# Query chunks split ahead of the second norm, transposes replaced by scaling matmuls, and modulation products kept back, in a decoder layer

## The chip, the cores and the metric

The kernel runs on one core of a Trainium2 chip. The metric is the device time of one execution in microseconds (us). Three runs of the kernel before took 1857.24, 1858.06 and 1858.55 us, a median of 1858.06.

The engines, by the names that the profile uses: PE is TensorE's matmul (PEld its weight load), DVE is VectorE, ACT is ScalarE, POOL is GpSimd, and SP is SyncE, which issues most of the loads. Each engine takes its instructions in the order in which they stand in its own list; an instruction that waits holds back all that stand behind it on that engine.

## What is computed

One layer of a decoder for 256 tokens of width 2048, all in float32. The parts that matter here:

```python
mod = (c_act @ w_ada[l] + b_ada[l]).reshape(B, 6, 1, D)
shift1, scale1, gate1, shift2, scale2, gate2 = jnp.moveaxis(mod, 1, 0)
h = rmsnorm(x, g_norm_mix[l]) * (1.0 + scale1) + shift1
q_a, ..., v_r, g_r = split_cols(h @ w_in[l], IN_SIZES)
o_nsa = ...                       # sparse attention, 16 heads of 64
o_ret = retention(..., g_r, ...)  # 8 heads of 128, silu(g_r) * normed output
x = x + gate1 * (jnp.concatenate([o_nsa, o_ret], axis=-1) @ w_out[l])
h2 = rmsnorm(x, g_norm_ffn[l]) * (1.0 + scale2) + shift2
x = x + gate2 * peer_ffn(h2, ...) # query product with peer_w_q, top-k, expert rows u and v
return rmsnorm(x, g_norm_final)
```

## The kernel before

Weights are streamed from HBM in chunks of 1 MB (128 partitions by 2048 floats). `load` issues such a chunk on SP into one of four `raw` buffers. `split_to` makes two parts of it: ACT copies it, rounded, to `whi` (L157), and DVE subtracts that from the chunk to get the remainder `wlo` (L158), each in two halves. Activations are kept split in the same way, as `hh` and `hl` in one tile `act`. A product is then three matmuls: hi by hi, hi by lo and lo by hi. There are two `whi` and two `wlo` buffers, so that two split chunks can stand ready.

The modulation `c_act @ w_ada` has 96 chunks (six vectors j of 16 chunks k). Each is a `raw` buffer that one DVE instruction multiplies with the broadcast row `crow` and sums (`ada_chunk`, L198, "the product"). They are spread over the whole first half of the program by `background(pace)`: a table PACE says how many of them stand behind each unit of other work (PACE["out"] behind each chunk of the output projection).

The stages around the change, in order of time:

- `d_pair` makes two rows of 128 of q and k of the input projection, in a bank `psD`. Its sum goes to `xT` by a DVE add (L430).
- `n_tile` makes 256 tokens by 512 columns in two banks `psN` from four chunks of 24 matmuls (L453): for the retention's values (`ret_v`), for its gates (`ret_gate`, which ACT turns to `sg` by a Silu, L633; there is one buffer `sg` for both halves of the heads), and later for the output projection (`woutN`, 16 chunks).
- `ret_head` runs a retention head: scores `scr`, decay `at` (L649), output `por`, its norm (L661 to L665). `ret_out` multiplies with the gate (`orr`, L672) and transposes (`psT`). `o_split` splits the output into `act` for the output projection (L677, L678).
- The output projection: four column tiles q. After each, for both token halves tt, DVE multiplies the bank with the gate row `g1` (`xg`, L719) and adds the residual (L720; the residual x is loaded into `xT`'s place, called x2, by eight loads on SP), and ACT squares and sums (L722).
- The second norm: `token_rstd` (a sum and a scaling on DVE, L215 and L216, and the power on POOL, L221), then eight DVE scalings `xn` (L731), 32 transposes on PE (`psX`, L736), evictions with the modulation's scale and shift on DVE and ACT in turn (L740, L742), and the split into `hh` (ACT, L743) and `hl` (DVE, L744).
- Then the first pools are closed and others opened. The 16 query chunks `wqT` follow: the first two in one loop (`t_blocks`, banks `psA`, L237 and L238), the others one by one, with ten more modulation products, the scores against the sub-keys, and the top-k on DVE. Behind these come the expert rows u (`psU`, L1111) and v (`acc`, L990), on PE without stop to the end.

The order of all instructions on an engine comes from a scheduler, by priorities (`tc.high_priority(offset=...)`) and readiness; `tc.keep_in_program_order` pins an instruction to the place in which it was written.

Of the kernel before, what the change touches and what calls it, by code (L numbers as in the profile page):

```python
# [30 lines left out]
PACE = dict(A=2, C=0.5, B=0.8, pair=1.5, tile=1.4, head=1.4, out=0.75)  # L31
# [84 lines left out]
def body(ctx, tc, a, out, dbg=None, stop=None):  # L116
# [8 lines left out]
    base = ctx.enter_context(tc.tile_pool(name="base", bufs=1))  # L125
    strm = []
# [26 lines left out]
    def split_to(r, hi, lo, parts=1):  # L153
        n = hi.shape[-1] // parts
        for i in range(parts):
            sl = slice(i * n, i * n + n)
            nc.scalar.copy(hi[:, sl], r[:, sl])  # L157
            nc.vector.tensor_sub(lo[:, sl], r[:, sl], hi[:, sl].bitcast(F32))  # L158

# [35 lines left out]
    def ada_chunk(j, k, crow):  # L195

        r = load(a["adaT"][j, k])
        nc.vector.scalar_tensor_tensor(r, r, 1.0, crow, op0=OP.mult, op1=OP.mult, accum_out=modc[:, j, k:k + 1])  # L198
# [29 lines left out]
    def t_blocks(pool, src_chunks, tags=("A", "A"), parts=2, dst=None):  # L228

        if dst:  # L230
            split_to(load(src_chunks[0]), *dst, parts)
        w = [dst] if dst else [split(load(c), parts=parts) for c in src_chunks]
        ps = [pool.tile([P, 2, S], F32, name="psA", tag=t) for _, t in zip(w, tags)]
        for k in range(KB):
            sl = slice(k * P, (k + 1) * P)
            for p_, (hi, lo) in zip(ps, w):
                nc.tensor.matmul(p_, hi[:, sl], act[:, k], start=k == 0, stop=False, skip_group_check=True)  # L237
                nc.tensor.matmul(p_[:, 1, :], lo[:, sl], hh[:, k, :], start=False, stop=k == KB - 1, skip_group_check=True)  # L238
        return ps

    def t_block(pool, src_chunk, tag="A", **kw):
        return t_blocks(pool, [src_chunk], (tag,), **kw)[0]

    def summed(ps, dst, n=S):

        nc.scalar.copy(dst, ps[:, 1, 0:n])
        nc.vector.tensor_add(dst, dst, ps[:, 0, 0:n])
# [31 lines left out]
    with ExitStack() as fctx:  # L279
        strm.append((fctx.enter_context(tc.tile_pool(name="strm", bufs=1)), dict(raw=4, whi=2, wlo=2)))  # L280
        fp = fctx.enter_context(tc.tile_pool(name="front", bufs=1))
        ones = fp.tile([P, P], F32, name="ones")
# [20 lines left out]
        kcv = fp.tile([P, 4, 2, P], F32, name="kcv", tag="f4k", bufs=2)  # L303
        ksw = [fp.tile([P, S], F32, name=f"ksw{i}") for i in range(4)]
        vsw = fp.tile([P, 2, 512], F32, name="vsw")
# [4 lines left out]
        pp = fctx.enter_context(tc.tile_pool(name="fpsum", bufs=2, space=PS))  # L310
# [17 lines left out]
        def background(n=1):  # L328
# [3 lines left out]
            for _ in range(n):  # L332
# [3 lines left out]
                ada_chunk(j, k, crow)  # L336
                if j == 0:
                    nc.vector.tensor_add(modc[:, 0:2, k], modc[:, 0:2, k], b_col[:, 0:2, k])
                    nc.vector.tensor_scalar(scol[:, 0, k:k + 1], modc[:, 1, k:k + 1], 1.0, g_mix[:, k:k + 1],
                                            op0=OP.add, op1=OP.mult)  # L340
                elif 1 < j < 5 and k == KB - 1:
                    nc.vector.tensor_add(modc[:, j, :], modc[:, j, :], b_col[:, j, :])
                    if j == 4:
                        nc.vector.scalar_tensor_tensor(scol[:, 1, :], modc[:, 4, :], 1.0, g_ffn, op0=OP.add, op1=OP.mult)
# [70 lines left out]
        kT2 = fp.tile([P, 4, 2, P], F32, name="kT2", tag="f4k", bufs=2)  # L415
# [27 lines left out]
        def n_tile(i, src="winN", tag="A", pace="tile"):  # L443
            ps = [pp.tile([P, 512], F32, name="psN", tag=tag) for _ in range(2)]
            for c in range(4):
                hi, lo = split(load(a[src][i, c].rearrange("p k e -> p (k e)")))
                for kk in range(4):
                    k = 4 * c + kk
                    w = slice(kk * 512, (kk + 1) * 512)
                    for tt in range(2):  # L450
                        ts_ = slice(tt * P, (tt + 1) * P)
# [910 lines left out]
```

## Time and profile before

| | |
|---|---|
| median of three runs | 1858.06 us |
| the profiled execution | 1856.91 us, its span 1855.2 us |
| matmuls on PE busy | 1793.1 us (97%) |
| DVE busy | 1485.7 us (80%) |
| ACT busy | 708.7 us (38%) |
| HBM read | 644.97 MB, 350 GB/s over the span |

A page of the profile has the busy times of the engines over the span, the chain of work that ended last (followed back from the last instruction, at each step to what released it), the costliest groups of instructions, and the waits. A row of a timeline reads: start, duration, engine, line, operation, what is written from what, and in brackets the engine's idle time before it with what ended it. A row of stretches reads: the stretch, its length, the busy time and count of PE, PEld, DVE, ACT and POOL, the granted clock of TensorE (1.00 is full), the DMA engines' busy share and GB/s. A row of waits reads: who waited, for whom, the sum in us, how often, the longest. A group's row reads: the line, engine, operation, names and shapes, how many, then busy us and mean ns, then the idle time before them.

### The profile page before, as it was taken

The page shows a single profiled execution, that of the slowest core. Times are in us where ns is not written, and L with a number is a line of the kernel's source. Part 1 is how long each engine was busy: PE and PEld are TensorE (multiplying, and loading weights), DVE is VectorE, ACT ScalarE, POOL GpSimd, SP SyncE. Part 2 cuts the span into 40 slices and gives each one's busy share as a digit, 9 for nine tenths or more (in the row PEclk, how much of TensorE's full clock was granted, in tenths as well). Part 3 has the DMA queues.
Part 4 walks back from the last instruction along what each step waited for, and adds up shares of the span by engine and source line. Part 5 has one row for each costly group of instructions (what it writes and reads, how often), then busy time and mean ns, then how long its engine had stood idle before and what let it go on. Part 6 is the DMA issues. An engine that isn't in the chain of part 4 may idle for free.

```text
span 1855.2 us, 28510 instructions
## 1 busy us (share of the span) xinstructions
PE 1793.1 (97%) x11264; PEld 1571.5 (85%) x11264; DVE 1485.7 (80%) x2336; ACT 708.7 (38%) x1284; POOL 366.1 (20%) x259
## 2 busy tenths in 40 slices
PE   5899999999889999999999999999999999999997
PEld 4899878797767899999997777779999998777775
DVE  7988889889779999586498999983555558998878
ACT  3444453745435421021045555541111114555554
POOL 1000001011010012211124434420111114544210
PEclk9999899999999999999999999999999999999999
DMA  8989887889887799999889999989999989999992
GB/s 341 409 320 362 313 308 292 342 302 334 318 338 279 278 322 364 424 366 376 332 346 386 423 420 416 409 355 425 367 345 359 354 316 404 426 421 403 388 316 99
DMA packets 94616, 653.96 MB, mean 353 GB/s; under 512 B 11409, under 2 KB 11633, under 8 KB 18449
## 3 DMA queue, kind: packets, MB, share of 16 engines
q1 hardware_dynamic: 66818, 467.78, 65.2%
q0 software_dynamic: 27664, 184.37, 25.3%
q8 instruction: 88, 1.44, 0.3%
q14 instruction: 46, 0.38, 0.1%
HBM read 644.97 MB, written 4.22 MB: 350 GB/s over the span
## 4 chain that ended last, share of the span: by engine, by line
PE 87%; DVE 7%; DMA 3%; issue 1%; ACT 1%; POOL 0%; SPq 0%; ACTq 0%; POOLq 0%; DVEq 0%
PE acc L990 31%; PE psU L1111 28%; PE psN L453 8%; PE psD L354 4%; PE psA L237 3%; PE bkB L354 2%; DMA raw<-in_adaT 2%; PE psA L238 1%; PE pg L1096 1%; DVE raw L198 1%; DVE wlo L158 1%; PE bkC L354 1%; PE bvB L406 1%; DMA raw<-in_winA 1%; PE pT L552 1%
## 5 line engine op out<-in xcount | busy, mean ns | idle before, releaser
L1111 PE MATMUL psU<-xT,raw 128*128 128x160 f32 x4096 | 569.5, 300 | 0.0
L1111 PEld LDWEIGHTS psU<-xT,raw 128*128 128x128 f32 x4096 | 558.3, 190 | 0.4
L990 PE MATMUL acc<-whi,cc 128*128 128x512 f32 x1512 | 369.1, 391 | 0.0
L990 PEld LDWEIGHTS acc<-whi,cc 128*128 128x128 f32 x1512 | 283.8, 188 | 70.0 <-issue 1.5
L967 DVE TENSOR_TENSOR wlo<-raw,whi 128x2048 fp32r<-128x2048 f32 x126 | 288.1, 2287 | 55.1 <-issue 47.4
L990 PE MATMUL acc<-wlo,cc 128*128 128x512 f32 x1008 | 254.2, 392 | 0.8 <-DVE wlo L967 0.6
L964 ACT CAST whi<-raw 128x2048 fp32r<-128x2048 f32 x126 | 240.7, 1911 | 0.5 <-DMA raw<-in_v 0.5
L198 DVE SCALAR_TENSOR_TENSOR raw<-raw,crow 128x2048 f32<-128x2048 f32 x96 | 219.0, 2283 | 19.7 <-DMA raw<-in_adaT 19.6
L157 ACT CAST whi<-raw 128x1024 fp32r<-128x1024 f32 (+1 forms) x174 | 168.5, 1018 | 167.1 <-DMA raw<-in_winA 32.4
L158 DVE TENSOR_TENSOR wlo<-raw,whi 128x1024 fp32r<-128x1024 f32 (+1 forms) x174 | 200.6, 1181 | 24.2 <-ACT whi L157 23.8
L990 PEld LDWEIGHTS acc<-wlo,cc 128*128 128x128 f32 x1008 | 161.5, 161 | 63.8 <-DVE wlo L967 3.1
L453 PE MATMUL psN<-whi,act 128*128 128x512 f32 x512 | 166.9, 402 | 1.4 <-ACT act L677 0.7
L1117 DVE TENSOR_TENSOR X<-X,ge 128x160 f32<-128x160 f32 (+19 forms) x94 | 25.8, 276 | 162.7 <-ACT ge L1116 160.5
L1113 ACT ACTIVATE X<-psU 128x160 f32<-128x160 f32 (+19 forms) x102 | 25.6, 251 | 315.6 <-PE psU L1111 299.6
L453 PEld LDWEIGHTS psN<-whi,act 128*128 128x128 f32 x512 | 95.9, 189 | 25.6 <-issue 1.7
L453 PE MATMUL psN<-wlo,act 128*128 128x512 f32 x256 | 103.3, 404 | 3.4 <-DVE wlo L158 3.4
L953 ACT CAST cc<-X 128x192 fp32r<-128x192 f32 x126 | 44.0, 352 | 148.1 <-PE acc L990 147.5
L237 PE MATMUL psA<-act,whi 128*128 128x512 f32 x240 | 87.2, 404 | 3.8 <-ACT whi L157 3.8
L806 POOL DMA_INDIRECT rows<-in_urow,sx x32 | 67.1, 2097 | 105.3 <-DVE rows L847 100.4
L806 POOL DMA_INDIRECT s<-in_urow,sx x26 | 53.9, 2072 | 120.6 <-DVE s L847 86.5
L354 PE MATMUL psD<-act,whi 128*128 128x256 f32 x384 | 75.4, 294 | 0.6 <-ACT whi L157 0.6
L969 ACT CAST cc<-cc 128x64 fp32r<-128x64 f32 x126 | 30.4, 243 | 117.2 <-DVE cc L954 117.2
(363 smaller groups left out, 2551.0 us busy)
## 6 DMA issues: line engine op xcount, KB each, us to landing
raw<-in_u SPq DMA_DIRECT2D x128, 1024.0 KB
raw<-in_v SPq DMA_DIRECT2D x128, 1024.0 KB
raw<-in_adaT SPq DMA_DIRECT2D x96, 1024.0 KB
raw<-in_winN SPq DMA_DIRECT2D x16, 1024.0 KB
raw<-in_woutN SPq DMA_DIRECT2D x16, 1024.0 KB
raw<-in_wqT SPq DMA_DIRECT2D x16, 1024.0 KB
raw<-in_winB SPq DMA_DIRECT2D x16, 832.0 KB
raw<-in_winD SPq DMA_DIRECT2D x12, 1024.0 KB
```

The source lines that it names most:

```text
L157: nc.scalar.copy(hi[:, sl], r[:, sl])
L158: nc.vector.tensor_sub(lo[:, sl], r[:, sl], hi[:, sl].bitcast(F32))
L198: nc.vector.scalar_tensor_tensor(r, r, 1.0, crow, op0=OP.mult, op1=OP.mult, accum_out=modc[:, j, k:k + 1])
L237: nc.tensor.matmul(p_, hi[:, sl], act[:, k], start=k == 0, stop=False, skip_group_check=True)
L354: nc.tensor.matmul(bank[:, b, :], x[:, w], y[:, k, :], start=k == k0 and n == 0 and first, stop=k == k1 - 1 and n == 2, skip_group_check=True)
L453: nc.tensor.matmul(ps[tt], x[:, k, ts_], y[:, w], start=k == 0 and j == 0, stop=k == KB - 1 and j == 2)
L806: pin(nc.gpsimd.indirect_dma_start(out=r, out_offset=None, in_=src, in_offset=bass.IndirectOffsetOnAxis(ap=o, axis=0)))
L953: inorder(nc.scalar.copy(ch, xb(j)))
L964: inorder(nc.scalar.copy(hi, r))
L967: nc.vector.tensor_sub(lo[:, i:i + n], r[:, i:i + n], hi[:, i:i + n].bitcast(F32))
L990: return nc.tensor.matmul(acc[c][0:m], x, w[:, c[1] * 512:(c[1] + 1) * 512], start=jj == 0 and n == 0, stop=jj == HALF - 1 and n == 2 - c[ ...
L1111: nc.tensor.matmul(ps, w[:, k * P:(k + 1) * P], xT[:, k, 0:TU], start=k == 0, stop=k == KB - 1)
```

## The change

1. The first three query chunks are loaded and split in the last column tile of the output projection. Their five parts stand in a pool `pre` (tile `w01`) that is opened where the attention's tiles (now in a pool `attn`) were, once that is closed behind the last `o_split`; the sixth takes the place of `crow`. So that this can be, the residual x is loaded to `xr`, in the place of `oT`, behind the last `o_split`.
2. One PSUM pool serves the whole kernel, with the same bank pairs.
3. In the last column tile the two token halves of the last two chunks are written one after the other (`apart=2`), and each half has its own `token_rstd`.
4. `xn` is gone: instead of transposing scaled rows, PE multiplies a slice of `xr` with a diagonal of the token half's factors (`dgs`, `turn_`). Eviction is as before; the split into `hh` and `hl` is made for two k at a time.
5. The matmuls of the first two query chunks are written between the turns, pinned in that order; the third chunk's stand behind them.
6. A modulation product (j of 2 or more) is kept back: its chunk is loaded where it was, and the DVE instruction stands pinned behind the next chunk's split.
7. PACE["out"] is 1.25 instead of 0.75. The ten products in the query loop stand at chunks 3 to 12 instead of 0 to 9, and each later query chunk is loaded and split one chunk ahead.

```diff
-PACE = dict(A=2, C=0.5, B=0.8, pair=1.5, tile=1.4, head=1.4, out=0.75)
+PACE = dict(A=2, C=0.5, B=0.8, pair=1.5, tile=1.4, head=1.4, out=1.25)
...
     def split_to(r, hi, lo, parts=1):
...
             nc.vector.tensor_sub(lo[:, sl], r[:, sl], hi[:, sl].bitcast(F32))
+        while pend_ada:
+            pend_ada.pop(0)(tc.keep_in_program_order)
...
     def ada_chunk(j, k, crow):
         r = load(a["adaT"][j, k])
-        nc.vector.scalar_tensor_tensor(r, r, 1.0, crow, op0=OP.mult, op1=OP.mult, accum_out=modc[:, j, k:k + 1])
+
+        def f(pin=lambda i: i):
+            pin(nc.vector.scalar_tensor_tensor(r, r, 1.0, crow, op0=OP.mult, op1=OP.mult, accum_out=modc[:, j, k:k + 1]))
+        return f
...
+def n_tile(i, src="winN", tag="A", pace="tile", apart=0):
...
             for c in range(4):
+                ws[c] = split(load(a[src][i, c].rearrange("p k e -> p (k e)")))
                 for kk in range(4):
                     for tt in range(2):
+                        if c < 4 - apart:
+                            mul(c, kk, tt)
                 background(pace)
+            for tt in range(2):
+                for c in range(4 - apart, 4):
+                    for kk in range(4):
+                        mul(c, kk, tt)
...
-        for q in range(4):
-            for tt in range(2):
-                nc.sync.dma_start(x2[:, tt, q * 512:(q + 1) * 512], a["x"][:, tt, q * 512:(q + 1) * 512])
         for k in range(12, KB):
             o_split(k, k + 1)
+        actx2.close()
+        w01 = fctx.enter_context(tc.tile_pool(name="pre", bufs=1)).tile([P, 5, D], F32R, name="w01")
+        xr = fp.tile([P, 2, D], F32, name="xr", tag="oT")
+        for q in range(4):
+            for tt in range(2):
+                nc.sync.dma_start(xr[:, tt, q * 512:(q + 1) * 512], a["x"][:, tt, q * 512:(q + 1) * 512])
...
             if q == 3:
                 background(len(todo))
+                settle()
+                w01 = [(w01[:, 2 * i, :], w01[:, 2 * i + 1, :] if i < 2 else fp.tile([P, D], F32R, name="w2l", tag="crow")) for i in range(3)]
+                for i, w in enumerate(w01):
+                    split_to(load(wq(i)), *w, 2)
...
+                    if q == 3:
+                        rcs.append(token_rstd(fp, ss[:, tt:tt + 1, :], 1, f"rc{tt}"))
+                        for rc in rcs if tt else []:
+                            dgs.append(fp.tile([P, P], F32, name=f"dg{len(dgs)}"))
+                            nc.vector.tensor_scalar(dgs[-1], ident, rc, None, op0=OP.mult)
...
-                    nc.vector.tensor_scalar(xn[:, tt, sl], x2[:, tt, sl], rc[:, tt:tt + 1], None, op0=OP.mult)
...
-                    nc.tensor.transpose(ps[:, tt, :], xn[:, tt, k * P:(k + 1) * P], ident)
...
+        def turn_(k, tt):
+            if tt == 0:
+                turned[k] = pp.tile([P, 2, 2, P], F32, name="psX", tag="TO"[k // 2 % 2])
+            for i in range(2):
+                tc.keep_in_program_order(nc.tensor.matmul(turned[k][:, i, tt, :], xr[:, tt, (k + i) * P:(k + i + 1) * P],
+                                                          dgs[tt], start=True, stop=True))
...
+            for tt in range(2):
+                for k in range(0, 8, 2):
+                    turn_(k, tt)
+            for k in range(0, KB, 2):
...
+                nc.scalar.copy(hh[:, k:k + 2, :], xT[:, k:k + 2, :])
+                nc.vector.tensor_sub(hl[:, k:k + 2, :], xT[:, k:k + 2, :], hh[:, k:k + 2, :].bitcast(F32))
+                for i in range(k, k + 2):
+                    t_block(first, w01[0:2], i, tc.keep_in_program_order)
+                if k + 8 < KB:
+                    for tt in range(2):
+                        turn_(k + 8, tt)
+        first += t_blocks(w01[2:], 2)
```

How the change moves instructions shows at three places. The first is PE's list where the output projection ends (psN) and the query product begins (psA); psX are the banks of the transposes or turns. Before:

```order
L453 MATMUL psN<-wlo,act 128x512
L453 MATMUL psN<-whi,act 128x512
L736 MATMUL psX<-small,xn 128x128 x32
L237 MATMUL psA<-act,whi 128x512
L238 MATMUL psA<-act,wlo 128x256
```

And now, where `dg` are the two diagonals and `w` the parts of the query chunks split ahead:

```order
L486 MATMUL psN<-whi,act 128x512
L791 MATMUL psX<-dg_4935,xr 128x128 x8
L791 MATMUL psX<-dg_4937,xr 128x128 x8
L260 MATMUL psA<-act,w_4277 128x512
L261 MATMUL psA<-act,w_4277 128x256
L260 MATMUL psA<-act,w_4277 128x512
L261 MATMUL psA<-act,w_4277 128x256
L260 MATMUL psA<-act,w_4277 128x512
L261 MATMUL psA<-act,w_4277 128x256
L260 MATMUL psA<-act,w_4277 128x512
L261 MATMUL psA<-act,w_4277 128x256
L791 MATMUL psX<-dg_4935,xr 128x128 x2
```

All 32 transposes stood ahead of the first query matmul; now 16 turns do, and the others stand two by two of each half between the query matmuls.

The second place is DVE's list at the same boundary. Before, from the last tile's residual on:

```order
L719 TENSOR_TENSOR xg<-psN,g_4420 128x512
L720 TENSOR_TENSOR xT<-xT,xg 128x512
L719 TENSOR_TENSOR xg<-psN,g_4420 128x512
L720 TENSOR_TENSOR xT<-xT,xg 128x512
L215 TENSOR_REDUCE rc<-ss 128x2
L216 TENSOR_SCALAR rc<-rc 128x2
L731 TENSOR_SCALAR xn<-xT,rc 128x512 x8
L740 TENSOR_SCALAR xT<-psX,scol,modc 128x256 x2
```

And now:

```order
L169 TENSOR_TENSOR w2l<-raw,w_4277 128x1024 x2
L772 TENSOR_TENSOR xg<-psN,g_4435 128x512
L775 TENSOR_TENSOR xr<-xr,xg 128x512
L233 TENSOR_REDUCE rc_4921<-ss 128x1
L234 TENSOR_SCALAR rc_4921<-rc_4921 128x1
L772 TENSOR_TENSOR xg<-psN,g_4435 128x512
L782 TENSOR_SCALAR dg_4935<-small,rc_4921 128x128
L775 TENSOR_TENSOR xr<-xr,xg 128x512
L233 TENSOR_REDUCE rc_4931<-ss 128x1
L234 TENSOR_SCALAR rc_4931<-rc_4931 128x1
L782 TENSOR_SCALAR dg_4937<-small,rc_4931 128x128
L802 TENSOR_SCALAR xT<-psX,scol,modc 128x256 x3
```

The first half's factors are made ahead of the second half's residual, and the splits of the three query chunks stand ahead of both. On PE the matmuls of the first half's last chunk end eight matmuls ahead of the last one.

The third place is DVE's list ahead of the two gate products (`orr<-orr,sg`) that release the one `sg` buffer for the second half of the heads. Before:

```order
L678 TENSOR_TENSOR act_70<-oT_90,act_70 128x2x256 x2
L158 TENSOR_TENSOR wlo_4161<-raw_4158,whi_4160 128x1024
L665 SCALAR_TENSOR_TENSOR bnb_3401<-bmv_3399,brs_3400 128x2
L158 TENSOR_TENSOR wlo_4161<-raw_4158,whi_4160 128x1024
L672 TENSOR_TENSOR orr_3377<-orr_3377,sg_3560 128x256
L678 TENSOR_TENSOR act_70<-oT_90,act_70 128x2x256
L198 SCALAR_TENSOR_TENSOR raw_4225,modc_65<-raw_4225,crow_95 128x2048
L672 TENSOR_TENSOR orr_3402<-orr_3402,sg_3560 128x256
```

And now:

```order
L169 TENSOR_TENSOR wlo_4294<-raw_4291,whi_4293 128x1024
L215 SCALAR_TENSOR_TENSOR raw_4228,modc_68<-raw_4228,crow_98 128x2048
L215 SCALAR_TENSOR_TENSOR raw_4324,modc_68<-raw_4324,crow_98 128x2048
L707 TENSOR_SCALAR brs_3377<-bmv_3376 128x2
L706 BN_AGGR bmv_3401<-bst_3400 128x2 x2
L722 TENSOR_TENSOR act_73<-oT_96,act_73 128x2x256
L707 TENSOR_SCALAR brs_3402<-bmv_3401 128x2
L169 TENSOR_TENSOR wlo_4332<-raw_4329,whi_4331 128x1024
L709 SCALAR_TENSOR_TENSOR bnb_3378<-bmv_3376,brs_3377 128x2
L709 SCALAR_TENSOR_TENSOR bnb_3403<-bmv_3401,brs_3402 128x2
L169 TENSOR_TENSOR wlo_4332<-raw_4329,whi_4331 128x1024
L215 SCALAR_TENSOR_TENSOR raw_4326,modc_68<-raw_4326,crow_98 128x2048
```

(The two gate products are the next two rows.) From the evacuation of the last projection pair (`xT<-cT,psD`) to the second gate product, two modulation products and four half splits stood before, and seven products and ten half splits stand now. Among them are already the splits of the output projection's first two chunks. On SP, the eight loads of x stood singly among the loads of `winN` and now stand together behind the sixth load of `woutN`.

More of the change, by code (lines that the diff above doesn't have):

```diff
@@ L226, in body, with t_blocks, t_block, summed @@
     hh, hl = act[:, :, 0, :], act[:, :, 1, :]
[L228 to L233, printed above, removed]
+    qbank = lambda i: f"b{(6, 7, 2, 3)[i % 4]}"
+    wq = lambda i: a["wqT"][i].rearrange("p k e -> p (k e)")
+    def t_blocks(w, i):
+        ps = [up.tile([P, 2, S], F32, name="psA", tag=qbank(i + n)) for n in range(len(w))]
         for k in range(KB):
[L235 to L238, printed above, removed]
-        return ps
[L241 to L247, printed above, removed]
+            t_block(ps, w, k)
+        return ps
+    def t_block(ps, w, k, pin=lambda i: i):
+        sl = slice(k * P, (k + 1) * P)
+        for p_, (hi, lo) in zip(ps, w):
+            pin(nc.tensor.matmul(p_, hi[:, sl], act[:, k], start=k == 0, stop=False, skip_group_check=True))
+            pin(nc.tensor.matmul(p_[:, 1, :], lo[:, sl], hh[:, k, :], start=False, stop=k == KB - 1, skip_group_check=True))
+    def summed(ps, dst, n=S, pin=lambda i: i):
+        pin(nc.scalar.copy(dst, ps[:, 1, 0:n]))
+        pin(nc.vector.tensor_add(dst, dst, ps[:, 0, 0:n]))
     def sumsq(wpool, kb, acc, src, tag="pr"):
@@ L732, in body @@
-        for k in range(KB):
-            with tc.high_priority(offset=(KB - k) * 10):
-                ps = pp.tile([P, 2, P], F32, name="psX", tag="TO"[k % 2])
-                for tt in range(2):
-                    nc.tensor.transpose(ps[:, tt, :], xn[:, tt, k * P:(k + 1) * P], ident)
-                t = xT[:, k, :]
-                ps = ps.rearrange("p t s -> p (t s)")
-                if k % 2:
-                    nc.vector.tensor_scalar(t, ps, scol[:, 1, k:k + 1], modc[:, 3, k:k + 1], op0=OP.mult, op1=OP.add)
-                else:
-                    nc.scalar.activation(t, ps, AF.Identity, bias=modc[:, 3, k:k + 1], scale=scol[:, 1, k:k + 1])
-                nc.scalar.copy(hh[:, k, :], t)
-                nc.vector.tensor_sub(hl[:, k, :], t, hh[:, k, :].bitcast(F32))
+                    nc.scalar.activation(sq, xr[:, tt, sl], AF.Square, accum_out=ss[:, tt, q:q + 1])
@@ new lines, in body @@
+                    if q == 3:
[3 more added lines that the diff above has]
+                            nc.vector.tensor_scalar(dgs[-1], ident, rc, None, op0=OP.mult)
+                nc.gpsimd.dma_start(x2d[:, tt, sl], xr[:, tt, sl])
+        first = [up.tile([P, 2, S], F32, name="psA", tag=qbank(i)) for i in range(2)]
@@ L758, in pair @@
             return t[:, 0, :], t[:, 1, :]
-        early = pair(0)
         X = []
```

150 lines of the change are left out of this document (87 added, 63 removed).

## The prediction

> **What bounds the kernel now.** First the page's busy times and the chain of work that ended last, then the busy times of chosen stretches.
>
> ```profile
> PE 1793.1 (97%) x11264; PEld 1571.5 (85%) x11264; DVE 1485.7 (80%) x2336; ACT 708.7 (38%) x1284; POOL 366.1 (20%) x259
> PE 87%; DVE 7%; DMA 3%; issue 1%; ACT 1%; POOL 0%; SPq 0%; ACTq 0%; POOLq 0%; DVEq 0%
> ...
> 446.00:545.00 99.00, 94.20 (x405) 74.76 (x404) 78.01 (x95) 40.43 (x60) 8.72 (x12) 0.98 0.88 328
> 545.00:576.00 31.00, 21.52 (x101) 17.00 (x101) 26.45 (x50) 16.79 (x37) 4.01 (x6) 0.78 0.71 274
> 660.00:703.00 43.00, 42.31 (x314) 41.49 (x313) 42.86 (x231) 10.46 (x21) 9.90 (x20) 1.00 0.92 327
> 703.00:760.00 57.00, 57.00 (x422) 57.00 (x422) 47.50 (x108) 7.54 (x18) 14.86 (x12) 1.00 0.95 388
> ```
>
> TensorE is the bound: 97% of the span, 87% of the chain. What can be won is its idle time, and that stands in two stretches that the change touches: 4.8 us of 99 in the output projection and 9.5 us of 31 behind it, where the granted clock is 0.78 besides. After 545 TensorE runs on with one small stop, so what is won or lost before is carried to the end. TensorE's waits between 400 and 720 say for whom:
>
> ```profile
> PE psX L736 <- DVE xn L731: 4.8, 1, 4.8
> PE psA L237 <- ACT whi L157: 3.8, 1, 3.8
> PE psN L453 <- DVE wlo L158: 3.4, 1, 3.4
> ...
> PE ptr L1240 <- DVE ex L1177: 0.7, 1, 0.7
> ...
> DVE raw L198 <- DMA raw<-in_adaT: 15.2, 8, 6.2
> ```
>
> The chain of waits from 477 on shows how the two largest groups come about:
>
> ```profile
> 477.77 6.39 DMA raw<-in_adaT
> ...
> 486.56 1.15 DVE wlo L158
> 487.75 56.62 PE psN L453 x235
> ...
> 546.44 0.70 DVE xT L720
> ...
> 548.43 0.72 POOL rc L221
> 549.17 0.50 DVE xn L731
> 549.81 1.94 PE psX L736 x8
> ```
>
> At 477.77 a modulation product on VectorE waits for its 1 MB transfer; the remainder (wlo) that TensorE needs stands behind it in VectorE's queue and comes at 486.56. At 545 the projection ends, and residual, sum of squares, power and eight scalings follow one another before TensorE has a transpose to do.
>
> **The change, part by part.** The sums are made against the profiled execution (span 1855.2, time 1856.91, 1.7 us around the span). The median of the runs shown is 1858.06, 1.15 above it, and I move that median by the difference that I find. T is the end of the projection's last matmul, 545.05 before.
>
> **1. The boundary behind T.** Rows of the tail and of the first query product before:
>
> ```profile
> 547.98 0.16 DVE L215 TENSOR_REDUCE rc<-ss 128x2 f32<-128x8 f32 x1 [0.85 <-ACT sq L722]
> ...
> 561.59 0.80 PE L237 MATMUL psA<-act,whi 128*128 128x512 f32 x1 [3.78 <-ACT whi L157]
> ...
> 574.65 0.39 PE L237 MATMUL psA<-act,whi 128*128 128x512 f32 x1
> ...
> 575.00 0.39 PE L237 MATMUL psA<-act,whi 128*128 128x512 f32 x1
> ...
> 554.00:556.00 2.00, 1.93 (x10) 1.31 (x9) 1.94 (x7) 2.00 (x6) 0.00 (x0) 0.51 0.95 394
> 556.00:558.00 2.00, 1.46 (x9) 0.74 (x8) 2.00 (x7) 2.00 (x7) 0.00 (x0) 1.00 0.10 37
> 564.00:566.00 2.00, 2.00 (x8) 1.71 (x7) 2.00 (x2) 0.38 (x1) 0.00 (x0) 0.50 0.32 94
> ```
>
> Two query chunks are 32 pairs of matmuls at 0.35 us (574.65 to 575.00): 11.2 us at full clock. They began at 561.59, 16.5 us after T, ran at half clock until 566, and ended near 575.1, T+30.
>
> After the change the first token half's sums close eight matmuls, 1.9 us, before T. On VectorE stand then, by the rows above: xg and xr (0.7 each, from T-1.9), the square's wait of 0.85, then sum, scaling and the power on GpSimd (1.2 from the sum's start to the next start on VectorE, 547.98 to 549.17). That makes the first rstd ready at T+1.6. Meanwhile xg of the second half has run; a diagonal of 128x128 follows and the first turn starts near T+2. The second half's xr ends at T+2.5; the same 0.85 and 1.2 and a diagonal (0.2, with its hand-over) follow: its turns start near T+5. The eight scalings xn are gone (TensorE waited for the first alone, 0.5), as is the wait of 3.78 for the first split, which is made before T.
>
> A turn is a matmul of f32 by f32, and the nearest rows of such are the scores; the evictions behind it are these:
>
> ```profile
> 581.05 0.89 PE pss L1138 x8
> ...
> L743 ACT CAST act<-xT 128x256 fp32r<-128x256 f32 x16 | 5.5, 409 | 0.0
> L742 ACT ACTIVATE xT<-psX,modc,scol 128x256 f32<-128x256 f32 x8 | 4.4, 566 | 3.9 <-PE psX L736 3.2 <-DMA x2d<-xT 0.7
> ...
> L744 DVE TENSOR_TENSOR act<-xT,act 128x256 fp32r<-128x256 f32 x16 | 5.8, 413 | 0.0
> L740 DVE TENSOR_SCALAR xT<-psX,scol,modc 128x256 f32<-128x256 f32 x8 | 4.2, 535 | 0.1
> ```
>
> Eight score instructions are four 128x128 products, two passes each: 0.22 us a turn, 0.44 at half clock. After the first pair's second-half turns (0.5 to 0.9) come an eviction (0.57), the copy of 512 (I take 0.65, between 0.41 for 256 and twice that) and the subtraction (0.68, as xr of 512): the first query matmul at about T+8.2. From there TensorE has 11.2 us of query pairs, 16 turns left at 0.22 (3.5), and the half clock, which before lasted 4.4 us (561.59 to 566) and so cost 2.2. A pair of chunks costs ACT 1.2 us and VectorE 1.2, against 2.3 on TensorE, so these hide. End: T+25.1 against T+30, **4.9 us won**. Bounds: if all turns run at half clock and the evictions are not hidden at the start, 3 less (1.9); if the clock doesn't fall, 2.7 more (7.6).
>
> [...]
>
> **2. The output projection.** Its 16 chunks have 24 matmuls each:
>
> ```profile
> 446.16 0.40 PE L453 MATMUL psN<-wlo,act 128*128 128x512 f32 x1
> 446.39 0.63 PE L453 MATMUL psN<-whi,act 128*128 128x512 f32 x2
> ...
> L198 DVE SCALAR_TENSOR_TENSOR raw<-raw,crow 128x2048 f32<-128x2048 f32 x13 | 29.8, 2290 | 11.7 <-DMA raw<-in_adaT 11.6
> ```
>
> At 0.2325 us from start to start (0.23 here) 384 matmuls are 89.3 us; the stage took 98.9 (446.2 to 545.05). The difference of 9.6 is 4.8 of stops, 3.4 of them behind the product's wait of 6.2, about 2 of half clock after it, and some 3 of the last heads' small matmuls. A product that stands behind the next chunk's split no longer holds that split back, so the 3.4 and its half clock should go: 5.4. Against that: two products more in the stage (14 for 12) and three more splits on VectorE, 2 x 2.29 + 6 x 1.15 (a half at 486.56) = 11.5 us, which its 21 us of idle time there (99 less 78) hide; 3 MB more of loads; the eight loads of x, which now wait for the last head's output and stand ahead of the seventh chunk's load on SyncE; and the residual's adds, which wait for them and stand ahead of a split on VectorE. I take 0.4 us of new stops: the stage at 93.9, **5.0 us won**. Bounds: 7 won with no stop at all, nothing won when the adds' wait takes the place of the product's.
>
> **3. The start of the output projection.** Here the order speaks against the change. The first output chunk's two banks come free when ACT has read the last gate tile, which it can only write when both gate products orr of the heads before have read its one buffer. Before:
>
> ```profile
> 418.33 0.28 PE L354 MATMUL psD<-act,wlo 128*128 128x256 f32 x1
> ...
> 423.02 0.68 DVE L430 TENSOR_TENSOR xT<-cT,psD 128x512 f32<-128x512 f32 x1
> ...
> 432.55 1.22 DVE L158 TENSOR_TENSOR wlo<-raw,whi 128x1024 fp32r<-128x1024 f32 x1
> 433.69 0.42 DVE L672 TENSOR_TENSOR orr<-orr,sg 128x256 f32<-128x256 f32 x1
> ...
> 434.63 2.28 DVE L198 SCALAR_TENSOR_TENSOR raw<-raw,crow 128x2048 f32<-128x2048 f32 x1
> ...
> 436.84 0.42 DVE L672 TENSOR_TENSOR orr<-orr,sg 128x256 f32<-128x256 f32 x1
> ...
> 445.16 1.30 ACT L633 ACTIVATE sg<-psN 128x512 f32<-128x512 f32 x2 [0.79 <-PE psN L453]
> ```
>
> The last projection pair was evacuated at 423.02 and the gate product came at 436.84, 8 us before ACT wanted the buffer: between them stood two products and four half splits. In the changed order seven products and ten halves stand there. VectorE reaches the evacuation earlier, but not before TensorE has made it: I take 416.5, from the pair's end at 418.6 and 2 us of head work that stands later now. Then 0.6 of evacuation, 7 x 2.21 (434.63 to 436.84) = 15.5, 10 x 1.14 (432.55 to 433.69) = 11.4, and some 9 of norms, decay and gate rows and o_split adds (an estimate: 22 rows by the 0.42 of orr): gate product at 453 and, with ACT's first write and one start, the first output matmul at 453.7 against 446.2: **7.5 us lost**. TensorE has nothing else to run there, for its own work up to this point is the same. Bounds: by the balance of work alone (five products and six halves more, 17.9, less what was done earlier, 423.0 to 416.5 and the 8 us of slack) 3.4 lost; nothing at all if VectorE sheds so much of its 15.2 us of waits for modulation chunks that it is ahead by then; at most 9, with the evacuation at 418.
>
> **4. After the boundary.** VectorE is 42.86 of 43 busy from 660 to 703 and TensorE waited 0.7 for it at the end. It sheds three splits (6 x 1.15 = 6.9), eight scalings (at most 0.5 each: 3 to 4) and 16 subtractions of 0.41 for 8 of 0.68 (1.2) behind T: some 11 us, against 4.9 that it must be earlier. So nothing is late next there; without that cover the gain of part 1 would be lost. The pools' change of place costs TensorE no instruction: nothing.
>
> Sum: 7.5 lost, 5.0 and 4.9 won: 2.4 us won, **1855.7**.
>
> **The rivals.** *The late start doesn't come* (part 3 costs nothing; VectorE gets ahead by the waits that it sheds): 9.9 won, 1848.2, to 1846 with the boundary's upper bound. For it: 15.2 us of waits for modulation chunks between 400 and 660 in the trace. Against: the rows that stand ahead of the gate product.
>
> *VectorE's queue takes the place of the product's wait* (the other side): the start is late by 8.8, and the adds of the first output tile wait for x and the gate row while the split of chunk seven stands behind them, so the 5.0 is not won either. From about 2 us of wait on it decides, as a chunk is 5.6 us and two split chunks are buffered. 8.8 - 4.9 = 3.9 lost, 1862.0, and with the boundary's lower bound 6.9 lost, 1865.
>
> *The boundary isn't shortened* (turns of two passes at half clock, VectorE's chain of two halves in one queue): part 1 gives 1.9, the sum is 0.6 lost, 1858.7.
>
> **How the numbers follow.** Forecast 0.46 (from 6 won to 1 lost), no late start 0.28, the queue 0.20, the boundary 0.06. What a measurement can tell from no change is 0.2%, 3.7 us. Faster by more: all of the second case and 0.17 of the first, 0.45. Slower by more: 0.15 of the queue's case and 0.02 of the last, 0.17. Within: 0.38. The range reaches from 1847, which leaves out a little of the second case, to 1864.5, which leaves out the queue's worst. The likeliest case alone reaches from 1852 to 1859.
>
> **What would show it.** Right: the first output matmul near 453 to 454 behind ACT's gate write, with TensorE idle some 9 us ahead of it; no stop of over 1 us between there and T; the first query matmul 8 us behind T, the third chunk's starting 25 behind; no wait for VectorE at the end of the selection. Wrong: an output projection that starts at 446 (second case), a stop on wlo in its second tile behind the add of x (third), turns of 0.44 us and a first query matmul later than T+11 (fourth).

## The result, and the profile after

The changed kernel takes 1882.71 us (median of four runs, 1881.24 to 1884.58) against 1858.3 us before: the ratio is 1.0121, with a 95% interval of 1.0102 to 1.0139. The forecast was 1855.7 with a range to 1864.5. The time is 18 us above the range and on the other side of no change.

The page's busy times and the chain that ended last, after the change:

```profile
PE 1801.2 (96%) x11296; PEld 1579.2 (84%) x11296; DVE 1483.5 (79%) x2324; ACT 705.8 (38%) x1274; POOL 362.1 (19%) x260
PE 77%; DVE 13%; DMA 6%; issue 2%; ACT 1%; POOL 1%; SPq 0%; ACTq 0%; POOLq 0%; DVEq 0%
```

PE is busy 8 us longer, part of it at half clock (0.50 from 502 to 508), and idle 16 us longer (78.2 for 62.1 us of the span). DVE's share of the chain has grown from 7% to 13%, that of transfers from 3% to 6%. PE's waits over the whole span say where:

```profile
PE por L696 <- ACT orr L711: 9.2, 1, 9.2
PE psN L486 <- ACT whi L168: 8.7, 4, 4.4
...
PE ptr L1306 <- DVE ex L1242: 4.7, 2, 3.3
...
PE psX L791 <- DVE dg L782: 2.7, 2, 2.1
```

The 4.8 and 3.8 us at the boundary and the 3.4 us in the output projection are gone. In their place stand one wait of 9.2 us ahead of the output projection, four waits of 8.7 us for ACT's splits, of which three with 7.0 us are in it, and 4.7 us at the end of the selection (`ptr`, the two transposes of the selected experts' numbers, behind DVE's last `ex`).

Three marks divide a span: ACT's first write of the second gate tile `sg` (the output projection starts 0.7 to 1.3 us later), T (the end of the projection's last matmul), and the first `ptr`. The table has all profiled runs that the text compares, in us; each column is the time from the mark ahead of it, and the first four add up to the span.

| kernel | start to sg | sg to T | T to ptr | ptr to end | span |
|---|---|---|---|---|---|
| before | 445.2 | 99.9 | 157.8 | 1152.4 | 1855.2 |
| changed | 456.5 | 109.4 | 160.2 | 1153.3 | 1879.4 |
| e1: products not kept back | 443.7 | 104.7 | 161.4 | 1153.8 | 1863.6 |
| e2: pace 0.75 | 456.0 | 100.6 | 170.9 | 1150.4 | 1877.9 |
| e4: before, products kept back | 459.5 | 99.7 | 162.3 | 1152.4 | 1873.8 |
| e5: x loaded by POOL | 456.9 | 111.8 | 160.2 | 1152.9 | 1881.8 |
| f5: e1, three products behind the turns | 446.2 | 103.5 | 160.0 | 1153.7 | 1863.4 |
| f6: f5, three more among the turns | 444.9 | 104.6 | 162.0 | 1156.2 | 1867.7 |
| f8: e1, pace 0.75 | 445.0 | 100.9 | 167.7 | 1146.2 | 1859.8 |
| f9: f8, query chunks' loads first | 450.2 | 102.1 | 171.2 | 1150.5 | 1874.0 |
| g2: e1, three raw buffers | 482.4 | 114.6 | 160.4 | 1148.1 | 1905.5 |
| d1: e1, ten products left out | 446.1 | 103.1 | 146.0 | 1157.0 | 1852.2 |

So the 24.2 us of the changed kernel's span are 11.3 ahead of the output projection, 9.5 in it, 2.4 from there to the end of the selection, although the boundary in that stretch became shorter, and 0.9 behind it.

**Ahead of the output projection.** A timeline of the changed kernel, of three engines in turn:

```profile
418.99 0.68 DVE L463 TENSOR_TENSOR xT<-cT,psD 128x512 f32<-128x512 f32 x1
...
455.71 0.76 DVE L716 TENSOR_TENSOR orr<-orr,sg 128x256 f32<-128x256 f32 x2
...
456.50 1.08 ACT L677 ACTIVATE sg<-psN 128x512 f32<-128x512 f32 x2 [1.28 <-DVE orr L716]
...
453.27 0.79 PE L696 MATMUL por<-vr,at 128*128 128x128 f32 x2 [9.20 <-ACT orr L711]
...
457.15 0.50 PE L486 MATMUL psN<-whi,act 128*128 128x512 f32 x1
```

DVE evacuates the last projection pair at 418.99 and comes to the gate products at 455.71; ACT waits for these (the bracket) and PE's first output matmul follows at 457.15, for 446.16 before.

**In the output projection.** ACT's row of waits (390 to 680 us) and SP's (440 to 680 us), of the changed kernel:

```profile
ACT whi L168 <- DMA raw<-in_woutN: 41.5, 11, 8.0
...
SPq L159 <- DVE wlo L169: 102.7, 19, 21.9
```

And SP's row of the kernel before:

```profile
SPq L148 <- DVE wlo L158: 65.8, 17, 18.3
```

DVE's wait for modulation chunks, 19.7 us over the whole span before, is 1.9 us now. ACT, which had no such wait among its largest there before, waits 41.5 us for the output chunks instead, and SP, which can issue a load only when the buffer is free, waits longer for the splits. PE's stretch from the first output matmul to T, first of the kernel before and then of the changed one, and PE's longest stop in it:

```profile
446.16:545.05 98.89, 94.08 (x405) 74.65 (x403) 77.90 (x95) 40.27 (x60) 8.56 (x12) 0.98 0.88 328
```

```profile
457.15:565.90 108.75, 100.06 (x407) 77.50 (x405) 82.03 (x105) 45.56 (x68) 7.09 (x12) 0.94 0.85 318
...
502.13 1.22 PE L486 MATMUL psN<-whi,act 128*128 128x512 f32 x2 [4.43 <-ACT whi L168]
```

PE stands idle for 8.7 us of it, for 4.8 before, and is busy 6.0 us longer, at a mean clock of 0.94 for 0.98.

**The boundary.** PE's timeline there:

```profile
565.50 0.40 PE L486 MATMUL psN<-whi,act 128*128 128x512 f32 x1
567.97 2.02 PE L791 MATMUL psX<-dg,xr 128*128 128x128 f32 x16 [2.07 <-DVE dg L782]
570.64 2.05 PE L791 MATMUL psX<-dg,xr 128*128 128x128 f32 x16 [0.64 <-DVE dg L782]
574.19 0.47 PE L260 MATMUL psA<-act,w 128*128 128x512 f32 x1 [1.50 <-issue]
...
591.21 0.39 PE L260 MATMUL psA<-act,w 128*128 128x512 f32 x1
```

And the stretch of the turns, with the granted clock third from the end:

```profile
568.00:572.00 4.00, 3.36 (x28) 3.17 (x29) 1.03 (x5) 1.33 (x4) 1.14 (x2) 1.00 1.00 387
```

T is 565.9. The turns start 2.1 us behind it, the second half's at 4.7, the first query matmul at 8.3; the first two chunks are through at 591.2, T+25.3, for T+30.3 before. The clock stayed at 1.00.

### The profile page after: what moved, and what is told of

It reads as the page before. It is cut to its first block, busy times and chain, and to the rows that moved or that the text cites. A ratio compares the mean times of both kernels' runs of the same rounds, so it can differ in the third digit from the quotient of the medians.

```text
span 1879.4 us, 28544 instructions
## 1 busy us (share of the span) xinstructions
PE 1801.2 (96%) x11296; PEld 1579.2 (84%) x11296; DVE 1483.5 (79%) x2324; ACT 705.8 (38%) x1274; POOL 362.1 (19%) x260
## 4 chain that ended last, share of the span: by engine, by line
PE 77%; DVE 13%; DMA 6%; issue 2%; ACT 1%; POOL 1%; SPq 0%; ACTq 0%; POOLq 0%; DVEq 0%
PE acc L1056 30%; PE psU L1177 24%; PE psN L486 6%; PE psA L260 3%; DVE raw L215 2%; PE bkB L387 2%; DVE wlo L169 2%; PE psD L387 2%; PE psA L261 1%; DMA raw<-in_woutN 1%; PE bkC L387 1%; PE bvB L439 1%; PE pg L1162 1%; DMA raw<-in_winN 1%; DMA raw<-in_adaT 1%
## 5 line engine op out<-in xcount | busy, mean ns | idle before, releaser
L168 ACT CAST whi<-raw 128x1024 fp32r<-128x1024 f32 (+1 forms) x170 | 164.7, 1019 | 181.7 <-DMA raw<-in_woutN 41.5
L169 DVE TENSOR_TENSOR wlo<-raw,whi 128x1024 fp32r<-128x1024 f32 (+1 forms) x170 | 195.5, 1183 | 45.3 <-ACT whi L168 43.1
L914 DVE SCALAR_TENSOR_TENSOR rows<-rows,h2t 128x2048 f32<-128x2048 f32 x32 | 73.1, 2285 | 7.5 <-DMA rows<-in_urow,sx 7.5
L873 POOL DMA_INDIRECT rows<-in_v,sx x25 | 62.0, 2480 | 75.8 <-DVE sp L920 63.5
L260 PE MATMUL psA<-act,whi 128*128 128x512 f32 x208 | 74.2, 398 | 0.0
```

The lines of the kernel that those rows point to most:

```text
L260: pin(nc.tensor.matmul(p_, hi[:, sl], act[:, k], start=k == 0, stop=False, skip_group_check=True))
L873: pin(nc.gpsimd.indirect_dma_start(out=r, out_offset=None, in_=src, in_offset=bass.IndirectOffsetOnAxis(ap=o, axis=0)))
L914: pin(nc.vector.scalar_tensor_tensor(r, r, 1.0, h, op0=OP.mult, op1=OP.mult, accum_out=d[:, e:e + 1]))
```

## The experiments

**e1: the products not kept back.**

```diff
-                    pend_ada.append(rest)
+                    rest()
```

> The changed kernel with the modulation products not kept back: each stands where its chunk is loaded, as before. Theory K (kept-back products cost the time: they stand ahead of the gate products, and each holds its raw buffer for one split longer, so that the next loads are issued late): the first output matmul comes 6 to 11 us earlier than 457.2, ACT's wait for woutN chunks falls from 41.5 to under 15 us, the output projection takes 99 to 102 instead of 108.7, and the time falls by 14 to 22 us, to 1861 to 1869. Theory X (the loads of x late and together, the pace of the loads, are what costs): the first output matmul 0 to 4 us earlier, the wait for woutN stays above 30 us, time within 6 us of the changed kernel, 1877 to 1883.

Measured: 1865.59 us, ratio to the kernel before 1.0027 (1.0017 to 1.0038). ACT's wait for the output chunks fell to 13.1 us and PE's 9.2 us ahead of the projection are gone. Theory K holds: 17 of the 24 us go with this one line. Two of its figures missed: the first output matmul comes 12 us earlier (445.1) and not 6 to 11, and the projection takes 104.7 us and not 99 to 102, so that half of its 9.5 us stay. In the lists of instructions, products that are kept back but not pinned give the order of e1 on every engine, so what does it is the pin. How the pin moves the gate products is open: they (L716) are written ahead of the output projection's chunks, and still stand behind splits and products of these in DVE's list. Raising their priority in the changed kernel left their place as it was.

**e4: that part alone, in the kernel before.** The edit is the change's `f(pin)` and `pend_ada`, pinned at the end of `split_to`, and nothing else of it.

> The kernel before with one part of the change alone: modulation products kept back and pinned behind the next split. Theory K: it alone makes the kernel before slower by 10 to 22 us, 1868 to 1880, with ACT waiting over 20 us for woutN or winN chunks (before: none of note). Theory X: within 4 us of before (1854 to 1862), or faster by up to 5 as the product no longer holds back the split that TensorE waits for.

Measured: 1872.86 us, ratio 1.0061 (1.0038 to 1.0085), 11 us slower. Its loss in the profiled execution is 14.3 us ahead of the output projection (459.5 for 445.2 in the table) and 4.5 behind it; the projection itself is not longer (99.7 for 99.9), though ACT waits 30.6 us for output chunks. So pinned products cost time by themselves ahead of the projection, and late output chunks cost PE nothing in it here. That the split chunks in store cover them was not tested.

**e2: the pace.**

```diff
-out=1.25)
+out=0.75)
```

> The changed kernel with the pace of the modulation chunks in the output projection at 0.75 as before, all else as changed. Theory K: the ring of four buffers is what fills, and fewer modulation chunks per output chunk free it only a little: 2 to 6 us faster than the changed kernel (1877 to 1881), the wait of ACT for woutN 25 to 40 us. Theory P (the pace itself crowds the loads): 8 us faster or more, the wait for woutN below 15 us.

Measured: 1881.80 us, 0.9 below the changed kernel. Neither theory's picture: ACT's wait for output chunks is still 33.4 us, as K has it, but the projection is 8.8 us shorter, as P would have it. The start of the projection is as late as in the changed kernel, and the chunks left over are loaded ahead of the query chunks, so the first diagonal stands on DVE behind their products and the query chunks' splits. PE's waits of this run:

```profile
PE psX L790 <- DVE dg L781: 11.4, 1, 11.4
```

The pace of 1.25 costs the projection some 9 us with pinned products and saves about as much behind it. In e1 and f8, without the pin, the same step is 3.8 us in the projection. Late chunks alone don't make a long projection: it takes 100.6 us here with 33.4 us of ACT's wait, and 104.7 in e1 with 13.1.

**e5: x loaded elsewhere.**

```diff
-                nc.sync.dma_start(xr[:, tt, q * 512:(q + 1) * 512], a["x"][:, tt, q * 512:(q + 1) * 512])
...
             ps = n_tile(q, "woutN", "AS"[q % 2], "out", 2 * (q == 3))
+            for tt in range(2):
+                nc.gpsimd.dma_start(xr[:, tt, sl], a["x"][:, tt, sl])
```

> The changed kernel with the loads of the residual x issued by GpSimd, two at each column tile, in place of eight together on SyncE ahead of the seventh output chunk. Theory X: the stop of 4.4 us at 502 and the half clock behind it go, output projection 6 to 9 us shorter, time 1874 to 1877. Theory K: the seventh chunk's load waits for its buffer all the same; 0 to 4 us faster, 1879 to 1883.

Measured: 1883.44 us, the projection 111.8 us for 109.4. Theory X falls: PE's wait for ACT's split in the projection is 8.7 us, for 7.0 in the changed kernel. The time is 0.7 us above that kernel's, where K had 0 to 4 us below.

**g2: three buffers in place of four.**

```diff
-dict(raw=4, whi=2, wlo=2)
+dict(raw=3, whi=2, wlo=2)
```

> On e1: three raw buffers instead of four in the first half of the kernel, products not kept back. Theory R (a product that is kept back costs above all because it holds a raw buffer, so that the next loads are issued late): the output projection looks as in the changed kernel, ACT waiting 30 to 50 us for woutN and the stage 106 to 112 us, time 1875 to 1895. Rival (the place of the products in VectorE's queue, not the buffers, is what costs): ACT's wait below 22 us, the stage at most 105 us, time below 1872.

Measured: 1907.57 us, beyond the forecast, as the stages ahead of the output projection lost 39 us too. ACT's wait for output chunks in this run:

```profile
ACT whi L168 <- DMA raw<-in_woutN: 50.4, 12, 14.4
```

The projection takes 114.6 us. One buffer less is enough for the picture that the changed kernel shows: late output chunks, with the products at their old place. This fits theory R, that a product kept back for one split longer takes a buffer away from the loads, but doesn't prove it: with a buffer less the stages ahead lost time too, and a fifth buffer in the changed kernel was not run.

**f5 and f6: the idle time behind the boundary.** In e1, PE's first matmul of the expert rows comes 3.7 us earlier than before, and its last 5.8 us later. PE's waits in e1 behind T, and then the stretch behind the second `ptr`, with the clock at 0.50:

```profile
PE ptr L1306 <- DVE ex L1242: 4.5, 2, 3.1
PE acc L1056 <- DVE wlo L1033: 3.2, 2, 2.6
```

```profile
750.00:752.00 2.00, 2.00 (x8) 2.00 (x9) 2.00 (x3) 0.37 (x1) 0.14 (x1) 0.50 1.03 434
```

DVE's timeline in e1 shows what precedes them:

```profile
570.21 2.36 DVE L169 TENSOR_TENSOR wlo<-raw,whi 128x1024 fp32r<-128x1024 f32 x2 [0.26 <-ACT whi L168]
578.94 1.08 DVE L266 TENSOR_TENSOR pq<-pq,psA 128x256 f32<-128x256 f32 x3 [6.37 <-ACT pq L265]
```

Behind the turns DVE splits one chunk and then stands 6.4 us for the first query sum, with a product and further splits behind it in its list. So products were moved into the gap:

```diff
-LATE = 6
+LATE = 6
+INSIDE = (4, 8, 12)    # f5: ()
+AFTER = 3
...
                         turn_(k + 8, tt)
+                if k in INSIDE:
+                    ada_chunk(5, LATE + INSIDE.index(k), crow)(tc.keep_in_program_order)
+        for k in range(AFTER):
+            ada_chunk(5, LATE + len(INSIDE) + k, crow)(tc.keep_in_program_order)
...
-            if 0 <= i - 3 < KB - LATE:
+            if 0 <= i - 3 < KB - LATE - 3:    # f6: - 6
```

> On the run without kept-back products (e1): three of the ten modulation products of the query loop moved to directly behind the turns, into VectorE's idle time there, and the third query chunk split in the ordinary buffers. Theory D (the rest of the loss is VectorE's idle time behind the boundary, 14 us more than before, which comes out at the end of the selection since VectorE works without a gap from there on): the end of the selection (first ptr) comes 5 to 7 us earlier than 709.8, TensorE's wait there falls, time 3 to 5 us below e1's 1865.6: 1860.5 to 1862.5. Theory L (the selection waits for its loads or for TensorE's scores): ptr moves by less than 2 us, time within 1.5 us of e1.

> As f5, with three further products pinned between the evictions of the turns, so that six of ten stand where VectorE idled. Theory D: first ptr 9 to 13 us earlier than 709.8, no wait of TensorE of over 1 us at either ptr, the boundary 0 to 2 us longer, time 6 to 10 us below e1: 1855.5 to 1859.5, level with the kernel before or faster. Theory L: no better than f5.

Measured: f5 1865.60 us, no better than e1, and f6 1870.88 us, worse. `ptr` comes at 709.7 in f5, for 709.8 in e1. In f5 PE no longer waits at `ptr` (0.3 us), but it has a new wait in the query product:

```profile
PE psA L262 <- ACT whi L170: 5.3, 1, 5.3
```

SP's timeline of f5:

```profile
574.89 0.33 SPq L161 DMA_DIRECT2D raw<-in_skT  x1
```

The first load of the next stage is issued at 574.89, for 539.73 in e1, behind the moved products, so that the next query chunk came late. As a way to use the gap this failed. The figures are those of theory L, but with a late chunk of the run's own making they do not tell D from L.

**d1: DVE relieved.** The ten products of the query loop are left out (the output lacks them); their chunks are still loaded.

```diff
-                ada_chunk(5, LATE + i - 3, crow2)()
+                nc.vector.tensor_copy(modc[:, 5, LATE + i - 3:LATE + i - 2], load(a["adaT"][5, LATE + i - 3])[:, 0:1])
```

> On e1: the ten modulation products of the query loop are left out (their chunks are still loaded; VectorE copies one column of each instead), so that VectorE has 22 us less to do between the boundary and the end of the selection. Theory D (VectorE's chain from the boundary to the selection's end costs e1 what the boundary had won): no wait of TensorE at either ptr, no half clock behind it, and the time 7 to 11 us below e1's 1865.6: 1854.5 to 1858.5. Theory L (what e1 loses there is loads or TensorE's own order): less than 3 us below e1.

Measured: 1855.98 us, ratio to the kernel before 0.9978 (0.9965 to 0.9990), 9.6 us below e1. PE's waits from 650 us on are two, none at `ptr`:

```profile
PE acc L1056 <- DVE pair L1033: 2.0, 2, 1.6
PE acc L1056 <- DVE wlo L1033: 0.6, 1, 0.6
```

Theory D holds for e1: between the boundary and the end of the selection it is bound by DVE's time. The ratio to the kernel before is not an even comparison, since that one still makes the ten products; the kernel before without them was not run.

**f8 and f9: e1 with the old pace.** f8 is e1 with `out=0.75`. In f9 the two chunks left over are loaded behind the query chunks and multiplied among the turns, and the third query chunk is split in the ordinary buffers:

```diff
-                background(len(todo))
-                settle()
...
+                w01.append(split(load(wq(2))))
+                left = [ada_chunk(*todo.pop(0), crow) for _ in range(len(todo))]
...
+                if k in (2, 6) and left:
+                    left.pop(0)(tc.keep_in_program_order)
```

> On e1: the pace of the modulation chunks in the output projection back at 0.75. If the pace of 1.25 crowds the loads of the output chunks (ACT still waits 13 us for woutN in e1): that wait under 6 us, output projection 2 to 4 us shorter, time 1861 to 1863.5. If not: the two chunks more at its end stand ahead of the query chunks' splits and of the sum; time 1865 to 1868.

> On f8 (no kept-back products, pace 0.75): the two modulation chunks left over are loaded behind the three query chunks, not ahead of them, and their products stand pinned among the turns; the third query chunk is split in the ordinary buffers. f8 lost 7 us at the boundary, where the first diagonal waited for splits of query chunks whose loads stood behind the two. If that order is the cause: first turn 2 to 4 us behind the end of the output projection instead of 7, the query product at 660 or before, time 1854 to 1859 (f8 1862), level with the kernel before or faster. If the boundary is limited by the query chunks' loads in any order: within 1.5 us of f8.

Measured: f8 1862.06 us, ratio 1.0013 (1.0003 to 1.0024), the lowest of the complete variants of the change (its interval overlaps with e1's) and still not faster than before. ACT's wait for output chunks fell to 3.3 us and the projection became 3.8 us shorter, as expected: the pace of 1.25 does crowd the loads. f9 took 1871.00 us. Its first turn still came 4.9 us behind T, PE waited 5.8 us for a query chunk's split as in f5, and 5.3 us at `ptr`. The expectation failed.

**h1, h2 and h3: the products on other engines.** The ten products of the query loop on POOL (multiply) and ACT (sum): h1 on e1, h2 on f8, h3 on the kernel before.

```diff
-                ada_chunk(5, LATE + i - 3, crow2)()
+                r, k = load(a["adaT"][5, LATE + i - 3]), LATE + i - 3
+                nc.gpsimd.tensor_tensor(r, r, crow2, op=OP.mult)
+                nc.scalar.activation(r, r, AF.Copy, accum_out=modc[:, 5, k:k + 1])
```

> On e1: the ten modulation products of the query loop made by GpSimd (multiply) and ACT (sum), both nearly idle there, in place of VectorE. Theory D (VectorE's chain from the boundary to the end of the selection takes back what the boundary won): no wait of TensorE at either ptr, time as where the products were left out, 1854 to 1859. Theory G (GpSimd's work on the same memory slows VectorE, or its 2048-wide multiply takes so long that the ring of buffers stops): TensorE's wait at ptr 3 us or more, time 1863 or above.

> The same on f8 (pace 0.75). f8 ends its output projection 3 us earlier than e1 but its boundary is 5 to 7 us longer. If VectorE's chain bounds it as well: 1854 to 1860. If f8 is bounded by its boundary, whose loss stays: 1860 to 1863, and h1 is the better of the two.

> The kernel before with the same ten products on GpSimd and ACT. Theory D: TensorE waited 0.7 us for VectorE at the end of the selection before, so that only that can go, and 8 us of its boundary are VectorE's and ACT's rows that stay: 1856 to 1860 (before 1858 to 1859). If it falls by 4 us or more, VectorE held the kernel before back somewhere that its trace doesn't show as TensorE's wait, and h1's gain isn't the boundary's.

Measured: 1888.81, 1885.96 and 1876.18 us, all slower. The groups of POOL and DVE in h1 (550 to 720 and 590 to 690 us):

```profile
L1258 POOL TENSOR_TENSOR raw<-raw,crow 128x2048 f32<-128x2048 f32 x10 | 48.9, 4895 | 33.9 <-DMA raw<-in_adaT 14.7 <-DVE twk L1188 7.6 <-DVE wlo L169 7.4
...
L169 DVE TENSOR_TENSOR wlo<-raw,whi 128x1024 fp32r<-128x1024 f32 x22 | 54.6, 2492 | 2.0 <-issue 2.0
```

And DVE's split in the same stretch of e1:

```profile
L169 DVE TENSOR_TENSOR wlo<-raw,whi 128x1024 fp32r<-128x1024 f32 x20 | 24.0, 1255 | 0.0
```

A product takes POOL 4.9 us in h1, and DVE's half splits there take 2.49 us for 1.26 in e1: what POOL took over, DVE lost again, and more. Theory G holds in the time, and in that DVE was slower with POOL at work; that the memory is what slows it, as the theory supposes, was not shown. The wait that it expected at `ptr` came earlier, as 20.0 us of PE's waits for DVE's splits in the query product. In h3 the half splits take 1.48 us in the same stretch (590 to 690), for 1.21 in the kernel before. Since DVE itself was slower in both, h1 and h3 say nothing of what a free DVE is worth; d1 does, for e1 alone.

## Why the prediction was wrong

**Part 1, the boundary: right in its times, one of them by luck.** Forecast were the first turns at T+2 and T+5, the first query matmul at T+8.2 and the end of two chunks at T+25.1; they came at 2.1, 4.7, 8.3 and 25.3. 4.9 us were forecast as won, and 5.0 were. That the end of the two chunks agrees is luck: the sum had put 2.2 us of half clock there, and the clock stayed at 1.00. In its place six pairs of the third chunk, 2.1 us, stand among the last pairs of the first two. This is the first of the six:

```profile
586.53 0.28 PE L261 MATMUL psA<-act,w2l 128*128 128x256 f32 x1
```

Measured to the end of the third chunk, the boundary is 7.0 us shorter (594.71 less 565.9, against 580.89 less 545.05), near the bound of 7.6 for a clock that doesn't fall. PE's idle time ahead of the turns was 2.1 us and not 4.8. The turns ran at full clock from the first on, 16 passes in 2.02 us.

**Part 3, the late start: right mechanism, its size off.** Forecast 7.5 us, measured 11.3 to ACT's write of the gate tile and 11.0 to the first matmul. The work between evacuation and gate products was sized well (36.5 us forecast, 418.99 to 455.71 measured). The evacuation came at 418.99 where 416.5 was taken, and the gate products' own time (0.76) was left out; together they put the loss beyond the forecast's bound of 9. The second rival's 8.8 is not worked out in the prediction. That the pin is what puts the gate products back (e1) was not seen.

**Part 2, the output projection: the step that failed first.** "A product that stands behind the next chunk's split no longer holds that split back, so the 3.4 and its half clock should go" was worth 5.4 us; the two products and 3 MB of loads more in the stage were put, with all else, at 0.4. Together 5.0 us were to be won, and the stage lost 9.5. The wait did go from DVE, and came back at ACT as a wait for the chunk's load. Four runs and the kernel before tell pin and pace apart (sg to T): 109.4 us with both, 100.6 with the pin at the old pace (e2), 104.7 at the new pace without the pin (e1), 100.9 with neither (f8), 99.9 before. At the old pace the pin thus costs the stage nothing, and wins nothing either. The pace of 1.25, which the forecast had taken as hidden, costs 3.8 us by itself, and the pin on top of it 4.7. Each of these figures is from one profiled execution.

Why the two add up so is argued and not shown: a product that stands one split later frees its raw buffer one split later, SP's next load waits for a buffer, and at the pace of 1.25 more loads want these buffers; g2 fits that. The forecast had counted instructions and queues and not how long each holds one of four buffers. The second rival had the right side, but not by its mechanism: moving the loads of x (e5) won nothing.

**Part 4, behind the boundary: the step that failed second.** "It sheds ... some 11 us, against 4.9 that it must be earlier. So nothing is late next there." DVE did shed that work, but stood idle in its place. The stretches from T to `ptr`, first of the kernel before and then of the changed one:

```profile
545.05:575.30 30.25, 20.78 (x96) 16.39 (x97) 26.00 (x48) 16.09 (x35) 4.01 (x6) 0.77 0.71 270
575.30:661.90 86.60, 86.60 (x522) 76.39 (x521) 85.47 (x293) 36.98 (x58) 2.11 (x4) 1.00 0.84 300
661.90:703.28 41.38, 40.69 (x306) 40.10 (x305) 41.24 (x226) 10.46 (x21) 10.10 (x21) 1.00 0.91 324
```

```profile
565.90:594.70 28.80, 24.58 (x160) 22.07 (x161) 14.06 (x26) 11.92 (x22) 3.38 (x6) 1.00 0.44 161
594.70:674.40 79.70, 79.70 (x478) 70.31 (x477) 76.79 (x219) 33.86 (x53) 2.64 (x5) 1.00 0.92 331
674.40:726.10 51.70, 50.28 (x378) 49.72 (x376) 51.55 (x298) 12.20 (x27) 9.90 (x20) 1.00 0.84 307
```

And DVE's timeline in the changed kernel:

```profile
595.19 1.08 DVE L266 TENSOR_TENSOR pq<-pq,psA 128x256 f32<-128x256 f32 x3 [6.37 <-ACT pq L265]
```

From T to `ptr` DVE's busy time fell from 152.7 to 142.4 us, 10.3 where some 11 were forecast. But its idle time grew by 12.3 us, and 10.5 of these lie in the first stretch, where it was busy 26.0 of 30.3 us before and 14.1 of 28.8 now. Its list has nothing ready in the gaps: three splits went ahead of T, the first modulation products went back by three chunks, and the first query sum is waited for (6.37 us) with the rest behind it. In the last stretch DVE works without a gap to speak of (51.6 of 51.7 us), so the gap came out at `ptr`: T to `ptr` became 2.4 us longer where PE had won 7.0. What the boundary won was lost at the end of the selection. d1 shows from the other side that DVE is the bound there: without the ten products T to `ptr` falls by 15.4 us against e1. Which of the changes behind T opened the gap was not tested one by one.

**The sum.** Forecast: 7.5 lost, 5.0 and 4.9 won. Measured: 11.3 and 9.5 lost, and the boundary's 7.0 won and given back with 3.3 more by the end (T to the end is 1313.5 for 1310.2). The range was worked out from bounds of the terms. Part 3 went beyond its bound, part 2 had the wrong sign and part 4 was put at nothing, and no bound allowed for these.

## What to carry to other kernels

Work that is put back in an engine's queue keeps what it reads: in a ring of few buffers a consumer that comes one step later makes a later load late, and the wait returns at another engine (30.6 us at ACT in e4). Whether that costs time depends on what else crowds the same loads, here the pace, so two such changes are to be sized together. A pin can move more than the instruction that it holds, so look in the engine's list for what comes to stand behind it, here the gate products that free the next banks. Time that an engine sheds is worth something only where its next work is ready; count the idle time that it leaves, and ask whether that engine is the bound further on.

## What the runs showed of the hardware

In h1, where POOL multiplies 128x2048 f32 in 4.9 us each, DVE's f32 subtractions of 128x1024 from 590 to 690 take 2.49 us, for 1.26 in e1. TensorE's clock stayed at 1.00 over an idle of 2.1 us behind T in the changed kernel, and stood at 0.50 behind one of 3.1 us at e1's second `ptr`. Behind the same idle of 2.54 us at T, 16 passes of the turns take 2.02 us in f5, as in the changed kernel at 1.00, and 32 take 5.44 in f6, where twice 2.02 is 4.04:

```profile
552.26 2.02 PE L794 MATMUL psX<-dg,xr 128*128 128x128 f32 x16 [2.54 <-DVE dg L785]
```

```profile
552.02 5.44 PE L794 MATMUL psX<-dg,xr 128*128 128x128 f32 x32 [2.54 <-DVE dg L785]
```

That the clock fell in f6 is an estimate from these times. If it did, the length of the idle time alone does not decide.
